# A group softmax streamed through six buffers: VectorE on tiles of two rows, VectorE and GpSimdE without loops, semaphore counts that only grow

## The chip, the cores and the metric

The kernel runs on one core of one Trainium2 chip. The metric is the device time of one execution in microseconds (us). All executions here were with a granted clock of 1.0.

## The reference

```python
B, N, D, G = 4, 4096, 4352, 8          # float32
x_g = x.reshape(B, N, 8, 544)
x_g = x_g - x_g.max(axis=-1, keepdims=True)
exp = np.exp(x_g)
out = exp / exp.sum(axis=-1, keepdims=True)
```

16384 rows of 4352 numbers, each row eight softmaxes of 544. In: 285 MB; out: 285 MB.

## The kernel before

A tile is 256 rows, two on each of 128 partitions (4352 KB). 64 tiles pass through six buffers. SyncE issues the loads and the last two stores, GpSimdE the other 62 stores. VectorE takes the maxima, ScalarE the exponentials and sums, VectorE the reciprocal and the product, all in place. VectorE does the maximum of the next row ahead of the scaling of this one.

```python
NT = 6; R = 2; S = R * NT              # six buffers of two rows: twelve row slots
def take(engine, sem, n=1):            # wait, then count down
    engine.sem_inc(sem, -n).wait_op(sem, n, "sem-ge")
def vector_max(n):                     # n is a row
    s = n % S
    i = nc.vector.reduce_max(out=mx[:, s, :], in_=row(s), axis=X, negate=True)
    if n == nr - 1:    i.wait_op(last_landed, 16, "sem-ge")
    elif s % R == 0:   i.wait_op(landed[s // R], 16, "sem-ge")
    i.then_inc(max_done, 1)
def vector_scale(n): ...               # reciprocal of 8 sums, product over 4352, per row
# [cut: ScalarE's exponentials, in a loop before and after]
for t in range(nt):                    # SyncE: loads
    if t >= NT: nc.sync.wait_ge(stored[t % NT], 16 * (t // NT))
    nc.sync.dma_start(...).then_inc(landed[t % NT], 16)   # the last tile as two halves
with nc.gpsimd.Fori(0, ring_turns) as u:                  # GpSimdE: stores
    for t in range(NT):
        take(nc.gpsimd, scaled, R)
        nc.gpsimd.dma_start(out=turn_out[u, t], in_=bufs[t][:, :]).then_inc(stored[t], 16)
vector_max(0)
with nc.vector.Fori(0, turns):
    for s in range(S):
        # [cut: counts of landed taken down by 16 once a turn]
        vector_max(s + 1)
        vector_scale(s)
    # [cut: counts of exp_done and rec_done taken down by S]
# [cut: the rows after the last turn, without a loop]
```

## Time and profile before

| | before |
|---|---|
| time, median of 3 | 1328.18 us (1328.03 to 1329.09) |
| span of the profiled execution | 1326.2 us |
| rate | 430 GB/s over the span, 433 in the middle |
| VectorE busy | 1207.7 us, 91% |
| instructions on record | 2968 |

The prediction shows the busy shares, slices, groups and the steady cycle. First the page's part on DMA issues: operation, engine, count, size, and the median us from issue to landing.

```profile
xt<-in_x_dram SPq DMA_DIRECT2D x63, 4352.0 KB, 41.4
out_dram<-xt POOLq DMA_DIRECT2D x62, 4352.0 KB, 51.1
```

A load takes 41.4 us and a store 51.1, although 4.46 MB at 433 GB/s are 10.3 us (an estimate). In the steady cycle one load and one store end every 20.6 us, so 41.4 and 51.1 us mean 2.0 loads and 2.5 stores under way at a time. I call these two numbers the depth of the two queues.

Then VectorE's end in order of time (start, duration, instruction, idle time ahead of it):

```profile
1262.90 4.69 DVE L66 TENSOR_REDUCE mx<-xt 128x8 f32<-128x4352 f32 x1 [1.70 <-DMA xt<-in_x_dram]
...
1293.94 4.68 DVE L66 TENSOR_REDUCE mx<-xt 128x8 f32<-128x4352 f32 x1 [2.65 <-DMA xt<-in_x_dram]
...
1304.89 4.69 DVE L78 TENSOR_TENSOR xt<-xt,rs 128x4352 f32<-128x4352 f32 x1
```

Tile 62 lands at 1262.9, the last half tile at 1293.9, and the last product ends at 1309.6, when the last store is issued.

### The profile page before, as it was taken

The page shows a single profiled execution, that of the slowest core. Times are in us where ns is not written, and L with a number is a line of the kernel's source. Part 1 is how long each engine was busy: PE and PEld are TensorE (multiplying, and loading weights), DVE is VectorE, ACT ScalarE, POOL GpSimd, SP SyncE. Part 2 cuts the span into 40 slices and gives each one's busy share as a digit, 9 for nine tenths or more (in the row PEclk, how much of TensorE's full clock was granted, in tenths as well). Part 3 has the DMA queues.
Part 4 walks back from the last instruction along what each step waited for, and adds up shares of the span by engine and source line. Part 5 has one row for each costly group of instructions (what it writes and reads, how often), then busy time and mean ns, then how long its engine had stood idle before and what let it go on. Part 6 is the DMA issues. An engine that isn't in the chain of part 4 may idle for free.

```text
span 1326.2 us, 2968 instructions
## 1 busy us (share of the span) xinstructions
DVE 1207.7 (91%) x384; ACT 764.5 (58%) x2049; POOL 33.3 (3%) x66
## 2 busy tenths in 40 slices
DVE  5999999999999898898998989989889898898984
ACT  3666565656565565555655556556565565555661
POOL 0000000000000000000000000000000000000000
DMA  9999999999999999999999999999999999999998
GB/s 403 420 432 431 435 433 429 434 435 437 433 427 435 436 434 435 426 437 435 434 434 427 437 436 433 431 432 437 435 433 429 433 436 437 432 429 434 436 433 356
DMA packets 18580, 570.47 MB, mean 430 GB/s; under 512 B 2064, under 2 KB 2064, under 8 KB 2064
## 3 DMA queue, kind: packets, MB, share of 16 engines
q1 hardware_dynamic: 9648, 294.13, 51.5%
q0 software_dynamic: 8928, 276.30, 48.3%
q14 instruction: 4, 0.03, 0.0%
HBM read 285.21 MB, written 285.21 MB: 430 GB/s over the span
## 4 chain that ended last, share of the span: by engine, by line
another core or an unknown queue 66%; DMA 7%; DVE 3%; SPq 1%; ACT 0%; issue 0%; POOLq 0%
DMA out_dram<-xt 4%; DMA xt<-in_x_dram 3%; DVE xt L78 1%; DVE mx L66 1%; SPq L109 1%; ACT xt L90 0%; DVE rs L75 0%; POOLq L124 0%
## 5 line engine op out<-in xcount | busy, mean ns | idle before, releaser
L90 ACT ACTIVATE xt<-xt,mx 128x544 f32<-128x544 f32 x1024 | 751.4, 735 | 539.1 <-DVE mx L66 539.1
L66 DVE TENSOR_REDUCE mx<-xt 128x8 f32<-128x4352 f32 x128 | 599.2, 4682 | 94.9 <-DMA xt<-in_x_dram 94.9
L78 DVE TENSOR_TENSOR xt<-xt,rs 128x4352 f32<-128x4352 f32 x128 | 600.6, 4692 | 4.4
L90 ACT ACTIVATION_READ_ACCUMULATOR xt<-xt,mx 128x1 f32 x1024 | 191.4, 187 | 0.0
L124 POOL DMA_DIRECT2D out_dram<-xt x62 | 33.1, 533 | 1239.9 <-POOLq L58 1239.9
L75 DVE RECIPROCAL rs<-sm 128x8 f32<-128x8 f32 x128 | 24.7, 193 | 2.6 <-ACT xt L90 2.6
L135 ACT ACT_TABLE_LOAD x1 | 1.3, 1283 | 1.0 <-SPq L51 1.0
L176 POOL MEMSET const-float32-0.0<- 128x1 f32 x1 | 0.1, 98 | 0.4 <-issue 0.4
L176 POOL MEMSET const-bfloat16-1.0<- 128x1 bf16 x1 | 0.1, 101 | 0.0
L176 POOL MEMSET const-float32-1.0<- 128x1 f32 x1 | 0.1, 98 | 0.0
L176 POOL MEMSET const-uint8-127<- 128x1 uint8 x1 | 0.1, 98 | 0.0
## 6 DMA issues: line engine op xcount, KB each, us to landing
xt<-in_x_dram SPq DMA_DIRECT2D x63, 4352.0 KB, 41.4
out_dram<-xt POOLq DMA_DIRECT2D x62, 4352.0 KB, 51.1
out_dram<-xt SPq DMA_DIRECT2D x2, 4352.0 KB, 19.3
xt<-in_x_dram SPq DMA_DIRECT2D x2, 2176.0 KB, 43.5
```

Of the source, the lines that this page charges most:

```text
L66: i = nc.vector.reduce_max(out=mx[:, s, :], in_=row(s), axis=X, negate=True)
L75: nc.vector.reciprocal(out=rs[:, s, :], in_=sm[:, s, :]).wait_op(exp_done, s + 1, "sem-ge").then_inc(rec_done, 1)
L78: nc.vector.tensor_tensor(out=xr, in0=xr, in1=rs[:, s, :].unsqueeze(2).to_broadcast([P, G, Dg]), op=mybir.AluOpType.mult,).wait_op(rec_don ...
L90: i = nc.scalar.activation(out=xr[:, g, :], in_=xr[:, g, :], func=Exp, bias=mx[:, s, g:g + 1], scale=1.0, accum_out=sm[:, s, g:g + 1],)
L109: nc.sync.dma_start(out=tile_in[:, :], in_=xt[t]).then_inc(landed[t % NT], 16)
L124: nc.gpsimd.dma_start(out=target, in_=bufs[t % NT][:, :]).then_inc(stored[t % NT], 16)
L135: nc.scalar.preload_act_table(Exp)
L176: nc = _bacc.Bacc("TRN2", target_bir_lowering=False, num_devices=1)
```

## The change

VectorE works a whole tile per instruction: one maximum, one reciprocal, one product for two rows, except in the last tile. Its code and GpSimdE's are written out without loops, and the semaphores are waited for at ever higher counts instead of being taken down. ScalarE keeps its loop, a tile a step.

```diff
+    parts = [(t, slice(0, RG)) for t in range(nt - 1)]
+    parts += [(nt - 1, slice(r * G, (r + 1) * G)) for r in range(R)]
     def vector_max(n):
-        s = n % S
-        i = nc.vector.reduce_max(out=mx[:, s, :], in_=row(s), axis=X, negate=True)
+        t, g = parts[n]
+        i = nc.vector.reduce_max(
+            out=mx[:, t % NT, g], in_=groups(t, g), axis=X, negate=True)
+        if g.start == 0:
+            i.wait_op(landed[t % NT], 16 * (t // NT + 1), "sem-ge")
     # [cut: reciprocal and product in the same way, waits at n + 1]
-    with nc.gpsimd.Fori(0, ring_turns) as u:
-        for t in range(NT):
-            store(t, turn_out[u, t])        # take(scaled, R), then the DMA
-    for t in range(steps, nt - LAST):
-        store(t, ot[t])
+    for t in range(nt - LAST):
+        nc.gpsimd.wait_ge(scaled, t + 1)
+        nc.gpsimd.dma_start(out=ot[t], in_=bufs[t % NT][:, :]).then_inc(stored[t % NT], 16)
-    with nc.vector.Fori(0, turns):
-        # [cut: the loop over S rows and the counts taken down]
-    for n in range(turns * S, nr):
-        if n + 1 < nr:
+    for n in range(len(parts)):
+        if n + 1 < len(parts):
             vector_max(n + 1)
         vector_scale(n)
```

More of the change, by code (lines that the diff above doesn't have):

```diff
@@ L20 @@
     NT = 6
-    S = R * NT
+    RG = R * G
     xf = x.flatten_outer_dims()
@@ L26 @@
     nt = N // (P * R)
-    nr = nt * R
-    turns = (nr - 1) // S
-    FIRST = 5
     LAST = 2
-    ring_turns = (nt - LAST) // NT
-    steps = ring_turns * NT
+    FIRST = 2
+    turns = (nt - 1 - FIRST) // NT
     f32 = mybir.dt.float32
@@ L37 @@
     ot = of.rearrange("(t p r) d -> t p (r d)", p=P, r=R)
-    turn_out = of[:steps * P * R, :].rearrange("(u b p r) d -> u b p (r d)", b=NT, p=P, r=R)
     landed = [tc.alloc_semaphore(f"landed{b}") for b in range(NT)]
     stored = [tc.alloc_semaphore(f"stored{b}") for b in range(NT)]
+    last_landed = tc.alloc_semaphore("last_landed")
+    last_stored = tc.alloc_semaphore("last_stored")
     max_done = tc.alloc_semaphore("max_done")
@@ L46 @@
     scaled = tc.alloc_semaphore("scaled")
-    last_landed = tc.alloc_semaphore("last_landed")
-    last_scaled = tc.alloc_semaphore("last_scaled")
-    last_stored = tc.alloc_semaphore("last_stored")
     ctx.enter_context(tc.tile_critical(no_gpsimd_drain=True))
     bufs = [ctx.enter_context(nc.sbuf_tensor(f"xt{b}", [P, R * D], f32)) for b in range(NT)]
-    mx = ctx.enter_context(nc.sbuf_tensor("mx", [P, S, G], f32))
-    sm = ctx.enter_context(nc.sbuf_tensor("sm", [P, S, G], f32))
-    rs = ctx.enter_context(nc.sbuf_tensor("rs", [P, S, G], f32))
@@ L57, in take @@
-    def take(engine, sem, n=1):
-        engine.sem_inc(sem, -n).wait_op(sem, n, "sem-ge")
-    def row(s):
-        b, r = divmod(s, R)
-        return bufs[b][:, r * D:(r + 1) * D].rearrange("p (g d) -> p g d", g=G)
-    def vector_max(n):
-        s = n % S
-        i = nc.vector.reduce_max(out=mx[:, s, :], in_=row(s), axis=X, negate=True)
-        if n == nr - 1:
+    mx = ctx.enter_context(nc.sbuf_tensor("mx", [P, NT, RG], f32))
+    sm = ctx.enter_context(nc.sbuf_tensor("sm", [P, NT, RG], f32))
@@ new lines, with groups @@
+    rs = ctx.enter_context(nc.sbuf_tensor("rs", [P, NT, RG], f32))
+    parts = [(t, slice(0, RG)) for t in range(nt - 1)]
+    parts += [(nt - 1, slice(r * G, (r + 1) * G)) for r in range(R)]
+    def groups(t, g):
+        return bufs[t % NT][:, :].rearrange("p (g d) -> p g d", d=Dg)[:, g, :]
+    def vector_max(n):
+        t, g = parts[n]
[3 more added lines that the diff above has]
+            i.wait_op(landed[t % NT], 16 * (t // NT + 1), "sem-ge")
+        else:
@@ L68, in vector_max @@
             i.wait_op(last_landed, 16, "sem-ge")
-        elif s % R == 0:
-            i.wait_op(landed[s // R], 16, "sem-ge")
         i.then_inc(max_done, 1)
     def vector_scale(n):
-        s = n % S
-        nc.vector.reciprocal(out=rs[:, s, :], in_=sm[:, s, :]).wait_op(
-            exp_done, s + 1, "sem-ge").then_inc(rec_done, 1)
-        xr = row(s)
+        t, g = parts[n]
+        nc.vector.reciprocal(out=rs[:, t % NT, g], in_=sm[:, t % NT, g]).wait_op(
+            exp_done, n + 1, "sem-ge").then_inc(rec_done, 1)
@@ L78, in vector_scale @@
+        xg = groups(t, g)
         nc.vector.tensor_tensor(
-            out=xr,
-            in0=xr,
-            in1=rs[:, s, :].unsqueeze(2).to_broadcast([P, G, Dg]),
+            out=xg,
+            in0=xg,
+            in1=rs[:, t % NT, g].unsqueeze(2).to_broadcast([P, g.stop - g.start, Dg]),
             op=mybir.AluOpType.mult,
-        ).wait_op(rec_done, s + 1, "sem-ge").then_inc(
-            scaled if n < (nt - LAST) * R else last_scaled, 1)
+        ).wait_op(rec_done, n + 1, "sem-ge").then_inc(scaled, 1)
@@ L86, in scalar_exp @@
     def scalar_exp(n, count):
-        s = n % S
-        xr = row(s)
-        for g in range(G):
+        t, gs = parts[n]
+        xg = groups(t, gs)
+        for g in range(gs.start, gs.stop):
             i = nc.scalar.activation(
-                out=xr[:, g, :],
-                in_=xr[:, g, :],
+                out=xg[:, g - gs.start, :],
+                in_=xg[:, g - gs.start, :],
                 func=Exp,
-                bias=mx[:, s, g:g + 1],
+                bias=mx[:, t % NT, g:g + 1],
@@ L95, in scalar_exp @@
                 scale=1.0,
-                accum_out=sm[:, s, g:g + 1],
+                accum_out=sm[:, t % NT, g:g + 1],
             )
-            if g == 0:
+            if g == gs.start:
                 i.wait_op(max_done, count, "sem-ge")
@@ L114 @@
                 ).then_inc(landed[t % NT] if r < R - 1 else last_landed, 16)
-    for k in range(LAST):
-        t = nt - LAST + k
-        nc.sync.wait_ge(last_scaled, (k + 1) * R)
+    for t in range(nt - LAST, nt):
+        nc.sync.wait_ge(scaled, t + 1 if t < nt - 1 else len(parts))
         nc.sync.dma_start(out=ot[t], in_=bufs[t % NT][:, :]).then_inc(last_stored, 16)
     nc.sync.wait_ge(last_stored, 16 * LAST)
-    def store(t, target):
-        take(nc.gpsimd, scaled, R)
-        nc.gpsimd.dma_start(out=target, in_=bufs[t % NT][:, :]).then_inc(stored[t % NT], 16)
-    with nc.gpsimd.Fori(0, ring_turns) as u:
-        for t in range(NT):
-            store(t, turn_out[u, t])
-    for t in range(steps, nt - LAST):
-        store(t, ot[t])
+    for t in range(nt - LAST):
+        nc.gpsimd.wait_ge(scaled, t + 1)
+        nc.gpsimd.dma_start(out=ot[t], in_=bufs[t % NT][:, :]).then_inc(stored[t % NT], 16)
     for t in range(nt - NT, nt - LAST):
@@ L140 @@
     with nc.scalar.Fori(0, turns):
-        for k in range(S):
+        for k in range(NT):
             scalar_exp(FIRST + k, k + 1)
-        nc.scalar.sem_inc(max_done, -S)
-    for k, n in enumerate(range(FIRST + turns * S, nr)):
+        nc.scalar.sem_inc(max_done, -NT)
+    for k, n in enumerate(range(FIRST + turns * NT, len(parts))):
         scalar_exp(n, k + 1)
     vector_max(0)
-    with nc.vector.Fori(0, turns):
-        for s in range(S):
-            if s == S - 1:
-                for b in range(NT):
-                    nc.vector.sem_inc(landed[b], -16)
-            vector_max(s + 1)
-            vector_scale(s)
-        nc.vector.sem_inc(exp_done, -S)
-        nc.vector.sem_inc(rec_done, -S)
-    for n in range(turns * S, nr):
-        if n + 1 < nr:
+    for n in range(len(parts)):
+        if n + 1 < len(parts):
             vector_max(n + 1)
```

## The prediction

> **What bounds the kernel now.** I read the page's busy shares and its 40 slices first.
>
> ```profile
> DVE 1207.7 (91%) x384; ACT 764.5 (58%) x2049; POOL 33.3 (3%) x66
> ...
> DMA  9999999999999999999999999999999999999998
> GB/s 403 420 432 431 435 433 429 434 435 437 433 427 435 436 434 435 426 437 435 434 434 427 437 436 433 431 432 437 435 433 429 433 436 437 432 429 434 436 433 356
> ...
> HBM read 285.21 MB, written 285.21 MB: 430 GB/s over the span
> ```
>
> VectorE looks like the limit at 91%, but the row of 9s under it says that the DMA engines never rest. The stretches view makes this exact. Its columns after the engines are the TensorE clock (not used here), the busy share of the 16 DMA engines, and GB/s.
>
> ```profile
> 60.00:284.00 224.00, 223.18 (x72) 141.67 (x381) 5.85 (x11) 1.00 1.00 433
> 284.00:1200.00 916.00, 840.70 (x268) 531.75 (x1427) 23.91 (x45) 1.00 1.00 433
> ```
>
> Up to 284 us VectorE works without a pause; after that it is 8% idle. The DMA share is 1.00 and the rate 433 GB/s in both, so an idler VectorE did not lower the rate and a fully busy one did not raise it. What VectorE waits for is in the groups:
>
> ```profile
> L66 DVE TENSOR_REDUCE mx<-xt 128x8 f32<-128x4352 f32 x128 | 599.2, 4682 | 94.9 <-DMA xt<-in_x_dram 94.9
> L78 DVE TENSOR_TENSOR xt<-xt,rs 128x4352 f32<-128x4352 f32 x128 | 600.6, 4692 | 4.4
> L75 DVE RECIPROCAL rs<-sm 128x8 f32<-128x8 f32 x128 | 24.7, 193 | 2.6 <-ACT xt L90 2.6
> ```
>
> It waits for loads (94.9 us), hardly for ScalarE (2.6 us). The steady cycle, in order of time (start, duration, instruction, and in brackets the idle time ahead of it):
>
> ```profile
> 602.97 4.69 DVE L66 TENSOR_REDUCE mx<-xt 128x8 f32<-128x4352 f32 x1 [1.61 <-DMA xt<-in_x_dram]
> 607.58 0.19 DVE L75 RECIPROCAL rs<-sm 128x8 f32<-128x8 f32 x1
> 607.80 4.69 DVE L78 TENSOR_TENSOR xt<-xt,rs 128x4352 f32<-128x4352 f32 x1
> 612.41 4.68 DVE L66 TENSOR_REDUCE mx<-xt 128x8 f32<-128x4352 f32 x1
> 617.01 0.19 DVE L75 RECIPROCAL rs<-sm 128x8 f32<-128x8 f32 x1
> 617.24 4.69 DVE L78 TENSOR_TENSOR xt<-xt,rs 128x4352 f32<-128x4352 f32 x1
> 623.55 4.69 DVE L66 TENSOR_REDUCE mx<-xt 128x8 f32<-128x4352 f32 x1 [1.62 <-DMA xt<-in_x_dram]
> ```
>
> A tile (two rows) takes 623.55 - 602.97 = 20.6 us, of which VectorE fills 18.9. A tile is 4352 KB in and 4352 KB out: 8.91 MB at 433 GB/s is 20.6 us. So the period is exactly the transfer time.
>
> Reading the trace's packet records one by one: all 16 engines are busy from 2.4 us to 1320.9 us, with one dip of 0.1 us near 1310; then one engine finishes alone, the last store lands near 1325, and the span ends at 1326.2. The time is therefore **2.4 start + 1318.5 solid transfer + 5.3 end**, and 2.0 us lie outside the span (1328.18 against 1326.2). The only way to change it by much is to change bytes, rate or the solidity of that block.
>
> [...] from 56 to 1256 us load and store queue have 49 to 51% each in 40 us stretches; while the last tile comes in as half-size packets, its loads fall to about a third. [...]
>
> **The change, part by part.**
>
> VectorE. 126 row maxima, reciprocals and multiplies become 63 of double length; the last tile keeps its two rows. [...] Starts follow one another 0.08 us before the profiled end (607.58 - 602.97 = 4.61 for a 4.69 instruction), so a long one costs 9.14 from start to start, and two cost 18.28; with a reciprocal of 0.23 a tile is **18.5 us, before 2 x (4.61 + 0.22 + 4.61) = 18.9**. Saved: 0.36 us x 63 = 23 us of VectorE time, all of it next to a 20.6 us transfer. The wait for loads grows from 1.7 to 2.1 us per tile instead. Worth on the path: 0.
>
> Loops and semaphores. Unrolling takes away branches and decrements on VectorE and GpSimdE; the pause between VectorE instructions inside a tile is already nothing, so again 0. Stores keep their 533 ns issue on GpSimdE, and ScalarE keeps 16 exponentials per tile (16 x 0.735 = 11.8 us, inside the 18.5 that follow its maximum).
>
> **The price: stores start later.** Before, the second row of tile t is finished after one maximum of tile t+1: the store is issued 613.22 - 602.97 = 10.3 us after tile t+1 landed. After, VectorE must do all of maximum t+1 and all of multiply t: 18.5 + 0.1 + about 0.5 issue lag as now = 19 us at most, I use 18.8. Stores are 8.5 us later against landings. Six buffers circulate: 6 x 20.6 = 123.7 us = load 41.4 + store 51.1 (medians from issue to landing) + 20.6 + 10.3 + 0.3. After, load + store must be 123.7 - 20.6 - 18.8 - 0.3 = **84 us, or 4.1 tiles in flight instead of 4.5**. Each direction alone at half the engines needs 20.6 us for a tile, so the queues still hold about two tiles each and the block stays solid. Nothing is lost in the middle.
>
> Start. Tile 0 lands at 13.97, maximum to 23.2, 16 exponentials to 35, reciprocal and multiply to 44.5: first store near 44.9 against 39.89. Six loads are 6 x 10.3 = 62 us of transfers, so the engines are busy until then without any store. Cost 0.
>
> End. Here work can lie open. Count from X, the landing of tile 62 (1262.9 before). Before, the last multiply ends at 1309.6, X + 46.7. After: long maximum 9.14, multiply of 61 with reciprocal 9.37, maximum of row 0 4.61, multiply of 62 9.37, so at X + 32.5 the last row's maximum starts (its load landed at X + 31 before, so VectorE and no longer the load decides); then the 15.7 us that this tail took before (1293.94 to 1309.6): **X + 48.2, 1.5 us later**. Where X itself falls follows from bytes: the engines are solid, so X is earlier by 10.3 us for each store tile still undone then. At X the store of tile 60 was issued 10.5 us ago before, about 2 us ago after. If the 8.5 us come wholly from the store queue, X is unmoved; wholly from the load queue, X is 8.5/20.6 x 10.3 = 4.2 earlier. Working the start forward (stores every 18.5 us, landings every 20.6, until VectorE first waits near tile 10 instead of 14) puts roughly 6 of the 8.5 on the stores, so X moves about 1.2 us earlier. Net: +1.5 - 1.2 = +0.3 us, and between 0 and +1.5.
>
> Sum: 1328.2 - 0 (VectorE) + 0 (middle) + 0.4 (end) = **1328.6 us**.
>
> **Rivals.** (1) VectorE is the bound and its saving counts: 23 us less, 1305 us. The 91% and the gap-free first 284 us speak for it; the equal 433 GB/s in both stretches and 94.9 us of waiting for loads speak against. (2) The later stores drain the six-buffer ring, and VectorE, loads and stores wait on each other in turn: if the engines lay idle only 0.3 us per tile, 19 us more, 1347 us. The coarser hand-over speaks for it, 84 us in flight against the 41 us that keep one tile in each direction moving speaks against. (3) The end only: VectorE's backlog leaves the engines idle before the last store by the full 1.5 us, perhaps with uneven engines on top: 1329.7 to 1332. The just-in-time dip at 1310 already shows this edge, so it is the likeliest miss. (4) Fewer tiles in flight make the transfers themselves quicker or slower by changing the mix; the rate at the start (loads alone), middle (mixed) and last 10 us (stores alone) shows engines at the same 100%, so I give it little.
>
> **Range and chances.** The three runs before span 1.1 us, so the low end is 1328.6 less 2. The high end takes rival 3 nearly whole. Range 1326.6 to 1331.8. Over 2% is 26.6 us either way: faster needs rival 1 in full, slower needs rival 2 at over 0.4 us a tile. Faster 0.01, same 0.97, slower 0.02.
>
> **What would show it.** Right: DMA share 1.00 and 433 GB/s from 60 to 1260 us; maximum and multiply near 9.22 us in 63 pieces each; VectorE near 1190 us busy, its wait for loads over 100 us; first store near 45 us; stores every 18.5 us until about 200 us, then every 20.6; store plus load latency near 84 us, the store losing more. Wrong: a DMA share under 0.99 in the middle, or a dip above 2 us before the last store.

## The result, and the profile after

| | before | after |
|---|---|---|
| time, median | 1328.11 us (4 runs, 1327.21 to 1329.09) | 1326.56 us (4 runs, 1326.47 to 1326.69) |
| ratio after/before | | 0.9988, 95% interval 0.9971 to 1.0006 |
| instructions on record | 2968 | 2463 |
| VectorE busy | 1207.7 us | 1190.0 us |

A ratio is the mean time of one kernel's runs over that of the other's runs of the same rounds, so not quite the ratio of the medians. The verdict at 2% is "same". The changed kernel is 1.55 us quicker, where 0.4 us slower was forecast, and it lies 0.04 us under the range. The interval of this one set includes 1. Two later sets gave 0.9989 and 0.9988; over all sets the kernel before never ran under 1327.1 us and the changed one never over 1326.9. So the small difference is real, although it is only 0.12% of the time.

Busy shares and slices of the changed kernel:

```profile
DVE 1190.0 (90%) x195; ACT 757.5 (57%) x2049; POOL 33.4 (3%) x66
...
DMA  9999999999999999999999999999999999999998
GB/s 404 421 432 436 428 435 434 434 431 433 433 435 433 432 434 433 436 429 435 432 436 431 433 433 434 434 431 435 433 436 429 435 432 436 431 432 434 433 431 372
```

The transfers are as solid as before; most of the gain shows only in the last slice (372 against 356 GB/s). The groups:

```profile
L61 DVE TENSOR_REDUCE mx<-xt 128x16 f32<-128x8704 f32 (+1 forms) x65 | 590.1, 9079 | 111.0 <-DMA xt<-in_x_dram 111.0
L74 DVE TENSOR_TENSOR xt<-xt,rs 128x8704 f32<-128x8704 f32 (+1 forms) x65 | 590.6, 9086 | 2.2
L71 DVE RECIPROCAL rs<-sm 128x16 f32<-128x16 f32 (+1 forms) x65 | 15.7, 242 | 2.8 <-ACT xt L85 2.8
```

VectorE's saving of 17.7 us turned into waiting: for loads it now waits 111.0 us instead of 94.9. The steady cycle:

```profile
598.18 9.22 DVE L61 TENSOR_REDUCE mx<-xt 128x16 f32<-128x8704 f32 x1 [1.97 <-DMA xt<-in_x_dram]
607.32 0.24 DVE L71 RECIPROCAL rs<-sm 128x16 f32<-128x16 f32 x1
607.60 9.23 DVE L74 TENSOR_TENSOR xt<-xt,rs 128x8704 f32<-128x8704 f32 x1
618.80 9.22 DVE L61 TENSOR_REDUCE mx<-xt 128x16 f32<-128x8704 f32 x1 [1.97 <-DMA xt<-in_x_dram]
```

The period is 20.6 us, as before. What did move is the depth of the queues:

```profile
xt<-in_x_dram SPq DMA_DIRECT2D x63, 4352.0 KB, 33.1
out_dram<-xt POOLq DMA_DIRECT2D x62, 4352.0 KB, 50.6
```

The sum is 83.7 us (84 was forecast), but of the 8.8 us given up the loads gave 8.3 and the stores 0.5. VectorE's end:

```profile
1257.81 9.22 DVE L61 TENSOR_REDUCE mx<-xt 128x16 f32<-128x8704 f32 x1 [2.02 <-DMA xt<-in_x_dram]
...
1290.38 4.68 DVE L61 TENSOR_REDUCE mx<-xt 128x8 f32<-128x4352 f32 x1
...
1301.33 4.69 DVE L74 TENSOR_TENSOR xt<-xt,rs 128x4352 f32<-128x4352 f32 x1
```

Tile 62 lands 5.1 us earlier than before, and the last store is issued at 1306.1 instead of 1309.6.

One more reading of the trace is needed, which no view prints. The trace has 16 semaphore increments for every transfer here (2064 for 129 transfers, before and after), and 16 packets of 4 bytes (the 2064 under 512 B on the page). I take each increment for the moment when one of the 16 engines was done with its part: the last one comes 0.47 us after the end of the last packet of a store (1324.36 and 1324.83 before, 1323.06 and 1323.53 after). That it stands for one engine is a reading of these counts and times; the trace does not name engines. The lag below is the last increment of a load behind the middle one (the eighth or the mean of the middle two), in us:

```
tile                4     10     16     26     44     56     62
before            1.55   1.60   1.52   1.45   1.99   2.78   3.23
after             0.56   1.06   0.98   1.24   2.04   2.61   2.86
```

**One engine falls behind the others**, by about 0.05 to 0.07 us per tile once it is the last one (tiles 44 to 56: 47 ns after, 66 ns before). The flat numbers ahead of that are those of another engine (see e7), which the growing one overtakes near tile 21 after and near tile 38 before. At the very end it works alone: from 1321.8 us on, the records of both executions have one data packet at a time. For the last store, the eighth engine posts at 1321.3 and the last at 1324.8 before; after, at 1320.8 and 1323.5. The span ends 1.4 us after that last increment in both. So the 1.3 us between the two spans (1326.2, 1324.9) lie in the landing of this one engine: 0.5 us the eighth engine gained as well, 0.8 us are a smaller lag (3.5 us before, 2.7 after).

### The profile page after: what moved, and what is told of

It reads as the page before. It is cut to its first block, busy times and chain, and to the rows that moved or that the text cites. A ratio compares the mean times of both kernels' runs of the same rounds, so it can differ in the third digit from the quotient of the medians.

```text
span 1324.9 us, 2463 instructions
## 1 busy us (share of the span) xinstructions
DVE 1190.0 (90%) x195; ACT 757.5 (57%) x2049; POOL 33.4 (3%) x66
## 2 busy tenths in 40 slices
DMA packets 18582, 570.48 MB, mean 431 GB/s; under 512 B 2064, under 2 KB 2064, under 8 KB 2064
## 3 DMA queue, kind: packets, MB, share of 16 engines
q1 hardware_dynamic: 9648, 294.13, 51.5%
q0 software_dynamic: 8928, 276.30, 48.3%
## 4 chain that ended last, share of the span: by engine, by line
another core or an unknown queue 69%; DVE 20%; DMA 7%; ACT 1%; SPq 1%; issue 0%
DVE xt L74 10%; DVE mx L61 10%; DMA out_dram<-xt 4%; DMA xt<-in_x_dram 4%; ACT xt L85 1%; SPq L104 1%; DVE rs L71 0%; SPq L166 0%; SPq L47 0%
## 5 line engine op out<-in xcount | busy, mean ns | idle before, releaser
L61 DVE TENSOR_REDUCE mx<-xt 128x16 f32<-128x8704 f32 (+1 forms) x65 | 590.1, 9079 | 111.0 <-DMA xt<-in_x_dram 111.0
L74 DVE TENSOR_TENSOR xt<-xt,rs 128x8704 f32<-128x8704 f32 (+1 forms) x65 | 590.6, 9086 | 2.2
L71 DVE RECIPROCAL rs<-sm 128x16 f32<-128x16 f32 (+1 forms) x65 | 15.7, 242 | 2.8 <-ACT xt L85 2.8
```

Source lines behind the costliest of these rows:

```text
L61: i = nc.vector.reduce_max(out=mx[:, t % NT, g], in_=groups(t, g), axis=X, negate=True)
L71: nc.vector.reciprocal(out=rs[:, t % NT, g], in_=sm[:, t % NT, g]).wait_op(exp_done, n + 1, "sem-ge").then_inc(rec_done, 1)
L74: nc.vector.tensor_tensor(out=xg, in0=xg, in1=rs[:, t % NT, g].unsqueeze(2).to_broadcast([P, g.stop - g.start, Dg]), op=mybir.AluOpType.mu ...
```

## The experiments

All gave correct results. Times are medians of five runs (six for e2 and e7). "before" ran in the same sets (medians 1328.08, 1327.86, 1328.17, 1328.33). The diffs are cut to the lines that matter; counts and waits that follow from them are left out. All these differences are far below 2%, so I compare medians and their scatter, mostly within a set.

### Set 1: the two parts alone, and tile 0

**c1_after**, the changed kernel as the control.

> The changed kernel again, as the control of this set. Three theories of the 1.5 us. EDGE: before, the last store is issued (1309.6) just as the engines run dry, and loses and scatters by 1 to 2 us; after, it is issued 3.5 us earlier and nothing runs dry. LAG: the end is set by one DMA engine that falls behind the others all through the run, and it falls behind less after (last landing 3.2 us behind the first against 3.6). NOISE: nothing but scatter of the kernel before. EDGE and LAG expect 1326.4 to 1326.8 in every run and before at 1327 to 1329; NOISE expects the two to overlap once each has more runs.

Measured: 1326.48 us (1326.38 to 1326.83), ratio 0.9989. NOISE is out: before, in 11 runs, had 1327.23 at the lowest.

**e1_rows_flat**: rows on VectorE, but no loops on VectorE and GpSimdE.

```diff
-            i.wait_op(landed[s // R], 16, "sem-ge")
+            i.wait_op(landed[t % NT], 16 * (t // NT + 1), "sem-ge")
-    with nc.gpsimd.Fori(0, ring_turns) as u: ...
+    for t in range(nt - LAST):
+        nc.gpsimd.wait_ge(scaled, (t + 1) * R) ...
-    with nc.vector.Fori(0, turns): ...
+    for n in range(nr): ...
```

> The change without its two-row tiles: one-row VectorE work as before, but no loops on VectorE and GpSimdE and counts that only grow. The first store comes at 39.9 as before, so the load latency stays near 41 us and the store latency near 51, and the last store is issued near 1309.6. EDGE expects the time of before, 1328.1 within 0.6. If loops or semaphore decrements cause the lag (one form of LAG): the time of after, 1326.6. If the count of VectorE instructions causes it: as before.

Measured: 1327.44 us (1327.30 to 1327.55). That lies between EDGE and the loops form of LAG. The stretches view, of 1308 to 1312 us (columns: VectorE, ScalarE and GpSimdE busy, clock, DMA share, GB/s):

```profile
1308.00:1312.00 4.00, 2.43 (x1) 0.00 (x0) 0.00 (x0) 1.00 0.71 305
```

The engines were visibly dry, because the last store was issued at 1310.5; yet the time is 0.6 us *under* that of before, where the same stretch has no such hole:

```profile
1308.00:1312.00 4.00, 1.58 (x1) 0.00 (x0) 0.00 (x0) 1.00 1.05 453
```

This is the first blow to EDGE.

**e2_tiles_loops**: two-row tiles, loops and decrements as before.

```diff
+    with nc.vector.Fori(0, vturns):
+        for s in range(NT): ...            # vector_max(s + 1), vector_scale(s, s + 1)
+    with nc.gpsimd.Fori(0, ring_turns) as u: ...
```

> The other part alone: two-row tiles on VectorE, with the loops and the decremented semaphores of before. First store near 45, load latency near 33, store latency near 51, last store near 1306. EDGE expects 1326.6, as after. LAG by loops or decrements expects 1328.1, as before; LAG by VectorE instruction count expects 1326.6.

Measured: 1327.21 to 1327.32 in four runs, 1334.31 and 1335.49 in two. The profile caught a slow one, at 428 GB/s over the span, with slices down to 423 in its middle (the changed kernel: 431, and no slice there under 428). Inconclusive; repeated as e11.

**e3_split_first**: the changed kernel with tile 0 in rows.

```diff
-    parts = [(t, slice(0, RG)) for t in range(nt - 1)]
+    parts = [(0, slice(r * G, (r + 1) * G)) for r in range(R)]
+    parts += [(t, slice(0, RG)) for t in range(1, nt - 1)]
```

> The changed kernel with only tile 0 worked in single rows, so that the first store goes out near 40 us instead of 45. If the time of the first store sets which queue gives up the depth: load latency back to about 43 us and store latency down to about 42 (sum still 84), tile 62 landing some 4 to 5 us later (1262) and the last store issued near 1310.5, past the edge. EDGE then expects the time to go back up to 1327.5 to 1329. LAG expects 1326.6 as after, since the slow engine still has work then. If the split is not set by the first store: latencies stay 33 and 51.

Measured: 1327.25 us (1327.18 to 1327.40), 0.77 over the control. I had built it badly for the first question: the long maximum of tile 1 still stands between the two rows of tile 0, so the first store came at 43.8 us, not near 40. The last store was issued at 1306.6 (control 1305.8), with no hole at 1310. EDGE cannot explain the 0.77 us; they lie again in the last engine, which posted its last increment at 1324.1 against 1323.2 in the control, with the eighth engine at 1320.7 and 1320.5.

### Set 2: what delays the last engine, and does a late store cost anything

**e4_pe_sems**: two thousand idle semaphore instructions on the unused TensorE sequencer.

```diff
+    for t in range(nt - LAST):
+        nc.tensor.wait_ge(scaled, t + 1)
+        for k in range(32):
+            nc.tensor.sem_inc(spare, 1 if k % 2 == 0 else -1)
```

> The changed kernel plus 62 x 33 semaphore instructions on the otherwise unused TensorE sequencer (two thousand more instructions; no data moved, no buffer touched, no other engine waits for them). In the four kernels run so far the DMA engine that finishes last falls behind at 0.046 to 0.073 us per tile, and the kernels with more instructions on record (2463, 2652, 2968) have the steeper slope; 505 instructions fewer went with 1.55 us less, about 3 ns each. If the count of instructions is what delays that engine: some 4 to 9 us more, 1330 to 1335. If not (the lag hangs on VectorE's or GpSimdE's own work or on the queues): 1326.5 within 0.3.

Measured: 1331.07 us (1330.97 to 1332.43), ratio 1.0026: 4.5 us more than the changed kernel in the other sets, for work that touches no data. The last increment comes at 1327.9, 5.9 us behind the eighth. The stretch 1322 to 1330 us of e4, then of the changed kernel:

```profile
1322.00:1330.00 8.00, 0.00 (x0) 0.00 (x0) 0.00 (x0) 1.00 0.04 18
```

```profile
1322.00:1330.00 8.00, 0.00 (x0) 0.00 (x0) 0.00 (x0) 1.00 0.00 1
```

One engine of 16 busy for the time is a share of 0.06; that is the lone engine. One thing was overlooked when e4 was planned, and again in the expectation of e8, which says that e4's instruction transfers were no more than in the changed kernel: the queue table of e4 has a queue that the changed kernel's lacks. The page gives its kind as instruction, and I take it to have brought in TensorE's code, since it is absent again when the same instructions stand in a loop (e8).

```profile
q8 instruction: 7, 0.11, 0.0%
```

e8 takes that away.

**e5_late_store**: the changed kernel with the last store made late.

```diff
+        if n == len(parts) - 1:
+            for k in range(2):             # outputs unused
+                nc.vector.reduce_max(out=junk[:, k, :], in_=..., axis=X, negate=True
+                ).wait_op(scaled, len(parts) - 1, "sem-ge")
```

> The changed kernel with two idle VectorE maxima (outputs unused) ahead of the last multiply, so that the last store is issued near 1310.5 instead of 1306, as late as in e1_rows_flat and later than in the kernel before. EDGE: fifteen engines dry by 1.5 to 2.2 us, the time up by as much, 1328 to 1328.7. LAG: the engine that finishes last still has work until about 1312, so the lateness is free: 1326.5 within 0.3, with a visible dip of the mean DMA share near 1310.

Measured: 1326.53 us median (1326.45 to 1326.70 and one 1327.88), the time of the changed kernel. The last store was issued at 1310.4, 4.4 us later than in the profile after. The stretch 1308 to 1312 us of e5, then of the changed kernel:

```profile
1308.00:1312.00 4.00, 2.41 (x1) 0.00 (x0) 0.00 (x0) 1.00 0.71 305
```

```profile
1308.00:1312.00 4.00, 0.00 (x0) 0.00 (x0) 0.00 (x0) 1.00 0.97 418
```

The hole is there and costs nothing: the eighth engine ends 1.3 to 1.6 us later than in the changed kernel's profiles (1322.1), the last one where it always did (1323.4). **EDGE is refuted.** The last engine, already 2.9 us behind the middle one at tile 62 of the changed kernel, must still have had older work when the store came.

**e6_rows_merge_first**: e1 with only tile 0 as one two-row tile.

```diff
+    parts = [(0, slice(0, RG))]
+    parts += [(t, slice(r * G, (r + 1) * G)) for t in range(1, nt) for r in range(R)]
```

> The row-wise kernel without loops (e1), with only tile 0 worked as one two-row tile, so that its first store goes out near 45 us instead of 39.3. If the time of the first store alone decides how the depth is shared: load latency down from 44 to about 33 us and store latency up from 49 to about 59 (rows hand over early, so the sum stays near 92.5), tile 62 landing near 1258, last store issued near 1305, no dip at 1310. LAG: the time stays at 1327.4, or moves only by what the start adds to the slow engine, under 0.8. EDGE: the time falls to 1326.5.

```profile
xt<-in_x_dram SPq DMA_DIRECT2D x63, 4352.0 KB, 33.0
out_dram<-xt POOLq DMA_DIRECT2D x62, 4352.0 KB, 59.7
```

The depths came out as forecast (33 and 59): the start alone shares them out. The time was 1326.60 us (1326.51 to 1326.65), 0.84 under e1 (of set 1; e1 came out the same in set 4, as e14). That is just above what I had allowed LAG and hits EDGE's number, but e5 of the same set excludes EDGE. So working tile 0 whole is worth some 0.8 us, and working tiles 1 to 62 whole is worth nothing: this row kernel is as quick as the changed one.

**e7_act_stores**: stores issued by ScalarE, ScalarE written out. In the changed kernel GpSimdE's 62 stores make up the 276.30 MB of the queue that the page calls software_dynamic; the loads and the last two stores, 294.13 MB, are on hardware_dynamic.

```diff
-        nc.gpsimd.wait_ge(scaled, t + 1)
-        nc.gpsimd.dma_start(...)
+    for n in range(len(parts)):
+        scalar_exp(n, n + 1)
+        t = n - 1
+        if 0 <= t < nt - LAST:
+            nc.scalar.wait_ge(scaled, t + 1)
+            nc.scalar.dma_start(...).then_inc(stored[t % NT], 16)
```

> The changed kernel with the 62 stores issued by ScalarE's hardware queue after the exponentials of the next tile, instead of by GpSimdE's software queue, and ScalarE without its loop; the bytes are the same. If the engine that lags does so [...]: its lag at the end falls from 2.7 us to below 1 and the time to about 1324.5 to 1325. If not: lag and time as in the changed kernel, 1326.2 to 1326.8.

What is tested is whether the lag falls when GpSimdE no longer issues them.

Measured: 1334.06 us (1333.88 to 1334.12 and one 1346.44), ratio 1.0065: a miss. The queue of kind instruction has 19 transfers, which I take for ScalarE's straight code being brought in:

```profile
q14 instruction: 19, 0.16, 0.0%
```

The changed kernel has 6 there. At most of these 8 KB transfers the lag of the last engine jumps by about 0.65 us and stays between them: 0.31 us are the transfer's own, and the data packet right behind it is some 0.31 to 0.35 us long in excess. The lag reached 10.9 us at tile 62. Writing out this loop was not free: 1334.06 us against 1326.84 with the loop kept (e10, of set 3).

The late engine of e7 is not the late one of the changed kernel. Most packets in the records start 3 or 4 ns before the end of another one, which I take for the packet ahead of it on its engine; so the packets around a code transfer can be strung together. In e7 the engine that carries the transfer is the last one of all at the end of the load under way, in at least 12 of the 19 (the transfer at 419 us: 4.4 us behind the median). In the changed kernel that is so for the transfers at 39 and 115 us, hence its step between tiles 4 and 10; but the engines with the transfers at 1169, 1218 and 1285 us are 0.1, 0.2 and 1.4 us behind, while the last one is 2.6 to 2.8. So code transfers are not what makes the changed kernel's last engine late in the end.

### Set 3: instructions or their code, which loop, and another queue

**e8_pe_loop**: e4's instructions in a small loop.

```diff
+    with nc.tensor.Fori(0, 31):
+        for k in range(64):
+            nc.tensor.sem_inc(spare, 1 if k % 2 == 0 else -1)
```

> As e4, two thousand executed semaphore instructions on TensorE's sequencer beside the changed kernel, but in a loop of 64 (31 turns, free running from the start), so that hardly any code has to be brought in. e4 cost 4.5 us, and its instruction transfers on record were no more than in the changed kernel. If executed instructions (or what is recorded of them) delay the slow DMA engine: about 4 us again, 1330 to 1331.5. If the delay came from bringing in e4's straight-line code by a way that the records don't show: 1326.4 to 1327.

Measured: 1329.89 us (1329.68 to 1330.98), 3.4 over the changed kernel, and the queue for TensorE's code is absent. The loop ran from the start until 316 us, and the lag shows it:

```
tile                4     10     16     26     44     56     62
after             0.56   1.06   0.98   1.24   2.04   2.61   2.86
e8_pe_loop        1.06   1.60   3.37   3.94   4.81   5.51   5.75
```

From tile 4 to 16 (62 to 309 us) it grows by 2.3 us against 0.4; afterwards by 0.05 us a tile, as elsewhere. So **executed instructions delay the last engine**, here by an estimated 3.4 us / 2049 more instructions on record = 1.7 ns each (1984 of them are the semaphore instructions, the rest is the loop's own); of e4's 4.5 us, about 1 us may belong to its code. The runs don't show by what way an instruction reaches a DMA engine; its recording is a candidate that they can't exclude.

**e9_pool_flat**: the kernel before with only GpSimdE's loop taken away.

```diff
-    with nc.gpsimd.Fori(0, ring_turns) as u: ...   # take(scaled, R), then the DMA
+    for t in range(nt - LAST):
+        nc.gpsimd.wait_ge(scaled, (t + 1) * R)
+        nc.gpsimd.dma_start(out=ot[t], ...)
```

> The kernel before, with only GpSimdE's loop and decrements taken away (its executed instructions fall from 298 to about 83; VectorE stays as before with loop and rows). Taking away both loops (e1) gave 0.6 us. If GpSimdE's instructions are what counts: 1327.4, as e1. If VectorE's: 1328.0, as before. If every instruction counts alike: about 1327.6.

Measured: 1327.38 us (1327.28 to 1327.56), as e1, and 0.79 under the median of before in its set. Taking away VectorE's loop as well (e1) adds nothing. The last increment is at 1324.2, against 1324.8 before. It also ends most of the scatter: 0.3 us between runs instead of the 2.5 us of before in that set. The two go together: three of before's nine runs there (1327.20, 1327.38, 1327.39) are as quick as e9. So the loop does not cost 0.79 us in every run; it costs from nothing to some 2 us, and 0.79 in the median.

**e10_act_loop_stores**: e7 with ScalarE's loop kept.

```diff
+    def store(t, target):
+        nc.scalar.sem_inc(scaled, -1).wait_op(scaled, 1, "sem-ge")
+        nc.scalar.dma_start(out=target, ...).then_inc(stored[t % NT], 16)
```

> As e7, the 62 stores on ScalarE's hardware queue and GpSimdE idle, but with ScalarE's loop kept, so that its code stays small. e7 showed 19 instruction transfers, each followed by a step of 0.65 us in the slow engine's lag, and no growth between them (elsewhere 38 to 67 ns per tile). If the software queue or GpSimdE's instructions make the steady growth: the lag at the end is 1 to 1.5 us and the time 1324.5 to 1325.5, under both kernels. If e7's flat stretches were chance: 1326.3 to 1327.

Measured: 1326.84 us (1326.67 to 1327.23): a miss. The last engine was 2.8 us behind at the end and growing by 45 ns a tile, as in the changed kernel, though GpSimdE issued no store at all (busy 0.00 us from 60 to 1330 us; the growth shows from tile 50 on; until then another engine is last). So GpSimdE's stores and their queue are not the cause, and e7's flat stretches were no evidence for it.

**e11_tiles_loops_again**: e2 unchanged.

> e2_tiles_loops once more, unchanged: four of its six runs took 1327.2 and two 1334 to 1335, and its profile was of a slow one. If the slow runs were a disturbance from outside: all or nearly all runs at 1327.2 to 1327.4, and a profile with a load latency of 33 us and a store latency of 51. If the kernel has two modes of its own: again about a third of the runs near 1334.

Measured: 1326.67 us (1326.52 to 1327.31), none near 1334. The slow runs of e2 did not come back, so I take them for a disturbance. But e2's good runs (1327.2) and e11's (1326.7) differ by 0.6 us for the same kernel, so in the presence of two-row tiles the loops of VectorE and GpSimdE together cost between 0.15 and 0.8 us, no more exactly known.

### Set 4: is the part of tile 0 real, and is it the time of the first store

**c2_after**, the control again.

> The changed kernel once more, as the control of this set. If the sets differ by more than 0.3 us for one and the same kernel, differences of that size between sets say nothing: so far it took 1326.56 and 1326.48.

Measured: 1326.50 us (1326.39 to 1326.77), ratio 0.9988. The changed kernel is the same in every set.

**e12_split_again**: e3 unchanged.

> e3 (tile 0 in rows, the rest as in the changed kernel) again. If rows in tile 0 cost something real: 0.6 to 0.9 us over the control of this set. If e3's 0.77 us was scatter of that set: within 0.3 of the control.

Measured: 1327.31 us (1327.25 to 1327.40), 0.81 over the control. Real.

**e13_rows_first_late**: e1 with its first store held back.

```diff
-        nc.gpsimd.wait_ge(scaled, (t + 1) * R)
+        nc.gpsimd.wait_ge(scaled, (t + 1) * R if t > 0 else R + 1)
```

> e1 (rows, no loops) with only its first store held back until row 2 is done, so that it is issued near 48.7 us instead of 39.3; VectorE's work is untouched. Which queue gives up the depth: 9.4 us later at the start, loads alone for that long, so a load latency down from 44 to some 25 to 27 us and a store latency up to about 66. The time: 1326.6, as e6, if it is the time of the first store that costs e1 its 0.8 us; 1327.4, as e1, if it is the rows.

```profile
xt<-in_x_dram SPq DMA_DIRECT2D x63, 4352.0 KB, 25.8
out_dram<-xt POOLq DMA_DIRECT2D x62, 4352.0 KB, 67.5
```

The depths followed the first store (48.7 us) as forecast. The time was 1328.58 us (1328.51 to 1329.41), over both forecasts. About 1 us of it is a wait at the close that e1 lacks; among the waits of SyncE's queue:

```profile
SPq L50 <- POOLq L50: 1.0, 1, 1.0
```

Without that, 1327.6 would be left, e1's time and not e6's. The last increment came at 1324.5, as in e1 (1324.4). So it is not the hour of the first store that costs the 0.8 us.

**e14_rows_flat_again**: e1 unchanged.

> e1 again in this set: 0.9 us over the control if the difference is real (1327.4), within 0.3 if it was scatter of the first set. Load latency 44, store latency 49, last store near 1310.5 with a dip, as in e1.

Measured: 1327.48 us (1327.43 to 1327.54), 0.98 over the control; last store at 1310.4. Real as well.

## Why the prediction was wrong

**Right.** The verdict "same", and the bound: the transfers stayed solid at 433 GB/s and the period at 20.6 us, and VectorE's saving was worth nothing. Its instructions took 9.22 us as forecast, it was busy 1190.0 us, the first store came at 44.9 us, the two latencies sum to 84 us. VectorE's tail from X, the landing of tile 62, to the last store took 48.2 us (1257.81 to 1306.05), as forecast. Rivals 1, 2 and 4 did not come about; of rival 3 the hole is seen in e1 and e5, but it costs nothing.

**Small slips in the working.** The 2.0 us "outside the span" mix two executions: the profiled one took 1327.87 us, so 1.7 lie outside. The sum books 0.4 us for the end where its working gives 0.3.

**Wrong without consequence: the share of the depth.** The step "puts roughly 6 of the 8.5 on the stores, so X moves about 1.2 us earlier" failed. The loads gave up 8.3 and the stores 0.5, and X moved 5.1 us, more even than the 4.2 that the prediction gave for that case. I had worked the start in rounded numbers, where half a tile decides. The rule that the runs show: as long as no store is out, the loads have all 16 engines, 10.3 us a tile (tiles 0 and 1 land at 13.96 and 24.27) instead of 20.6, so each us by which the first store is later takes about 2 us off the load latency for good. At tile 13 that latency is 45.7 us for a first store at 39.3 (e1), 35.5 for 43.8 (e3), 32.2 for 44.7 (c1), 25.7 for 48.7 (e13). VectorE first waited regularly near tile 13, not 10, for the same reason. Yet e5 shows that issuing the last store 4 us later does not matter, so the 3.5 us by which it came earlier are not what made the time shorter.

**Wrong, and the cause of the miss: the fixed end.** "2.4 start + 1318.5 solid transfer + 5.3 end" put the lone engine's 3.5 us into a constant, and the step "Net: +1.5 - 1.2 = +0.3 us, and between 0 and +1.5" let the time depend on when the last store is issued. That is the step that failed: with the last store issued at 1310.4 instead of 1306.1 the time was the same (e5). The time depends on one engine that falls behind through the run, and this lateness moves with things that I had set to 0:

- "Loops and semaphores ... so again 0": GpSimdE's loop costs 0.79 us in the median of the kernel before, and much of its scatter (e9). The other loop and VectorE's fewer instructions gave no gain that these runs resolve (e9 to e1; e6 against the changed kernel). That executed instructions can delay the last engine is shown by e8; that it is GpSimdE's 215 instructions fewer which do it here is argued from that, and only in part: at e8's 1.7 ns they would be worth an estimated 0.4 us.
- "Start ... Cost 0": tile 0 worked whole instead of in rows saves 0.77 and 0.81 us (e3 against c1, e12 against c2), with the last engine's increment 0.7 to 0.9 us earlier. The hour of the first store is not the reason (e13), nor the hour of the last (e5), nor the number of code transfers, which is 6 in e3 and in the changed kernel, 7 in e1 and in e6. **What is, stays open.**

The two, 0.79 and about 0.8, add up to 1.6 of the 1.55 measured. As a sum this is only fair: measured in the other order (e11, e2), the part of the loops is 0.15 to 0.8 us.

The range failed as well: it allowed 2 us below the forecast, although the base was a kernel whose own runs scatter over more than that (1327.1 to 1329.7 over all sets), and rival 3 looked only upwards.

## What to carry to other kernels

Here the transfers were solid from start to end (433 GB/s, a DMA share of 1.00). Shortening VectorE's work by 17.7 us, off that path, bought nothing of its own (e6, with rows in tiles 1 to 62, takes 1326.60 us, the changed kernel 1326.56), and issuing the last store 4.4 us later was free too (e5). So look at which of the 16 DMA engines lands last, and by how much (3.5 and 2.7 us behind the eighth here), before treating start and end as constants. How the six buffers shared their depth between loads and stores was fixed by how long the loads ran alone at the start, some 2 us of latency for each us (45.7 to 25.7 us for a first store 9.4 us later). Below 1% of the time, the number of executed instructions (e8: 0.26%) and the size of unrolled code (e7: 0.57%) were terms of their own, so an experiment needs its control in the same set, and a median alone says little of a kernel whose runs scatter.

No version tried is quicker than the changed kernel; e6 and e11 equal it within 0.2 us.
